# Strassen's seven products for half of the product with w_out in a hybrid decoder layer

## The chip, the cores and the metric

The kernel runs on one core of one Trainium2 chip. The metric is the device time of one execution in microseconds (us); the time of a kernel is the median of its runs. Engines are named as the profile names them: PE is TensorE (matrix products; PEld its weight loads), DVE is VectorE, ACT is ScalarE, POOL is GpSimd, SP issues the loads.

## The reference

One decoder layer over 256 tokens of 1024 channels, in float32: a SwiGLU block, then an SSD branch and a differential attention branch side by side, merged by gates, then a second SwiGLU block. The change is in the line that multiplies the merged branches by `w_out`, and its neighbours:

```python
def rmsnorm(x, g):
    xf = x.astype(jnp.float32)
    y = xf * lax.rsqrt(jnp.mean(xf * xf, axis=-1, keepdims=True) + EPS)
    return y.astype(x.dtype) * g

    ...
        merged = gates[:, :, 0] * y_ssd + gates[:, :, 1] * y_att
        h = h + rmsnorm(merged @ w_out[l], mix_post_g[l])
        h = h + 0.5 * rmsnorm(swiglu(rmsnorm(h, ffn2_pre_g[l]), ffn2_w_gate[l], ffn2_w_up[l], ffn2_w_down[l]),
                              ffn2_post_g[l])
```

`merged` is 256 x 1024 and `w_out` 1024 x 1024.

## The kernel before

**Number format.** Products run in TensorE's rounded float32. To keep float32's precision every operand is split into a high part (rounded) and a low part (the rest), and a product is the sum of three: high x high, low x high, high x low. For weights ScalarE makes the high part (`whi`, L259) and VectorE the low part (`wlo`, L260), each in two operations of 128x1024 for a chunk of 1 MB. For activations ScalarE casts and VectorE subtracts in `split` (L320, L321).

**Weights.** All chunks stand in one list in the order of their use. `load_to` (L241) issues a chunk's load on SP's queue when one of three raw buffers comes free, which is when the low part of the chunk three places earlier has been made. `take` hands the next unit's split weights to the products and splits those up to `AHEAD` = 3 units ahead. The split weights and most activations lie in a pool of 29 tiles (`k4`); small ones in pools of 4 and 7 (`k3`, `k2`). PSUM's eight banks are a pool of three (`pj`) and one of five (`bg`).

**Order.** From the gates on, TensorE's queue is in the order in which the program states it (`own_order(PE)`); the other engines' orders are made by a scheduler when the program is built. An engine works off its own order, and where its next instruction waits, all behind it wait.

**The stage.** The two branches' products (`pws`, `pwd`) leave TensorE in halves of 512 channels and blocks of 128 tokens. VectorE multiplies such a tile by its gate (L1612) and adds the other branch's (L1613), in place in `gt`. `turn_merged` has TensorE transpose a merged tile (`pmg`, L1596) and splits the result into `mh` and `ml`, the activations of the product with w_out. The first half's two tiles are turned after the first weights of the second half's `pwd`, the second half's two within the product with w_out.

`mm_n` computes that product: `acc[b][q]` is the 128-token block b and the 512-column half q, four banks of `bg`. The chunk of the first 256 channels is multiplied for both blocks at once, with the two later transposes between its steps; the other three chunks (`TAIL` = 3) are held, first for block 0, then for block 1:

```python
        for q in range(2):
            for i, w in held:
                one(i, w, ((0, (q,)),), late=not norms or q == 1 or i < n - 1)
```

`ready(0)` then computes block 0's norm while TensorE does block 1: the squares on ScalarE (L506), the gain product on VectorE (`og`, L605), the root on GpSimd (L511, L512), h on VectorE (L645). `turned` has TensorE transpose block 0's h (`pu_f`, L520) ahead of the last third of the stage, for FFN2's first products (`pn_f`); block 1's h is normalized (`un_f`, L565) and transposed within them.

**Strassen elsewhere.** Both SwiGLU blocks' down products already use seven products for eight on three groups of 512 channels each. `Quad` makes the sums of weight quarters on VectorE (`wt`, L122), their high part on ScalarE (`wqh`, L130) and low part on VectorE (`wql`, L136); `sums_of` makes the sums of activation quarters (`sv`, L737 to L740) and splits them (`sh`, `sl`, `s`).

Of the kernel before, what the change touches and what calls it, by code (L numbers as in the profile page):

```python
# [47 lines left out]
SSD_US = 1.55  # L48
DOWN = {"f1": "q1 p q2 p q3 ppp", "f2": "q1 p q2 p q3 ppp"}
FIRST, LAST = (1, 2, 3, 5, 7, 6, 4), (1, 6, 7, 2, 3, 5, 4)  # L50
BREAK, STOP = object(), object()


@with_exitstack
def tile_hybrid_layer(ctx: ExitStack, tc: tile.TileContext, x, ffn1_pre_g, ffn1_w_gate, ffn1_w_up,
# [33 lines left out]
    def bg(shape, name):  # L89
        return ps.tile(shape, F32, tag="bg", name=name, bufs=5)  # L90


    class Quad:
# [32 lines left out]
        def split(self, p):  # L126
            load_to(self.i + 2)
            hi = k4([P, 2, 512], f"wqh{self.i}{p}", F32R)
            src = self.quarter(self.PLAIN[p], p) if p in self.PLAIN else self.sum_of(p)
            nc.scalar.copy(hi, src)  # L130
            rest = self.products[self.products.index(p) + 1:]
            for later in rest[:1] + tuple(q for q in rest[1:2] if p == 3 and q == 4):
                if later in self.SUMS:
                    self.sum_of(later)
            lo = k4([P, 2, 512], f"wql{self.i}{p}", F32R)
            nc.vector.tensor_sub(lo, src, hi.bitcast(F32))  # L136
            self.give_back()
            return lambda kt: hi[:, kt, :], lambda kt: lo[:, kt, :]
# [74 lines left out]
    for c in range(2):  # L213
        for k0 in (0, 512):
            s_chunk(da_w_branch[0], k0, c * 512)
    for c in range(4):
        n_chunk(w_out[0], c * 2 * P)
    ffn_chunks("f2", ffn2_w_gate, ffn2_w_up, ffn2_w_down)

# [187 lines left out]
    def act_table(name):  # L407
        f = nc.scalar.preload_act_table_set(name)
        for prev in act_since:
            tc.add_manual_dep(f.ins, prev, order, reason="activation table")  # L410
        act_since.clear()
        act_fence[0] = f.ins.name
# [317 lines left out]
    def sums_of(g, even, odd):  # L730
# [11 lines left out]
        split(more[:, 0], more[:, 1], v[:, 3])  # L742
        return ([hi[:, i] for i in range(3)] + [more[:, 0]], [lo[:, i] for i in range(3)] + [more[:, 1]])

    def mm_quads(acts, sums, tag):


        bank = {p: bg([P, 512], f"acc_{tag}p{p}") for p in (2, 3, 5, 4, 8)}
        bank.update({p: pj(f"acc_{tag}p{p}") for p in (1, 6, 7)})
        acc = [[bank[2], bank[3]], [bank[4], bank[8]]]  # L750
        begun, n_quads = set(), max(n for n, (kind, j) in enumerate(down[tag]) if kind == "q") + 1
        of_quads = down[tag][:n_quads]

        def mm(p, x_, w_, last):
            nc.tensor.matmul(bank[p], x_, w_, start=p not in begun, stop=last and p in (1, 5, 6, 7))  # L755
            begun.add(p)

        for n, (kind, j) in enumerate(of_quads):
            last = n == n_quads - 1
            if kind == "p":  # L760
                wh, wl = take()
                for kt in range(2):
                    ah, al = acts[2 * j + kt]
                    for b in range(2):
                        ts = slice(b * P, (b + 1) * P)
                        for x_, w_ in ((ah, wh), (al, wh), (ah, wl)):
                            for q in range(2):
                                p = ((2, 3), (4, 8))[b][q]
                                mm(p, x_[:, ts], w_(kt)[:, halves[q]], False)
                continue  # L770
            sh, sl = sums[j]
            for p in LAST if last else FIRST:
                wh, wl = take()
                for kt in range(2):
                    if p in (1, 2, 4):
                        k, b = {1: (0, 0), 2: (2, 0), 4: (2, 1)}[p]
                        ah, al = (x_[:, b * P:(b + 1) * P] for x_ in acts[4 * j + k + kt])
                    else:
                        ah, al = (x_[{5: 0, 6: 1, 7: 2, 3: 3}[p]][:, kt, :] for x_ in (sh, sl))
                    for x_, w_ in ((ah, wh), (al, wh), (ah, wl)):  # L780
                        mm(p, x_, w_(kt), last and kt == 1 and w_ is wl)
            sums[j] = None
        p1, u2, u3, u4, c4 = (k2([P, 512], f"{n}_{tag}") for n in ("p1", "u2", "u3", "u4", "c4"))
        add = lambda o, a, b: nc.vector.tensor_tensor(o, a, b, ALU.add)

        def combine():
            nc.scalar.copy(p1, bank[1])
            m = add(u2, bank[6], p1)
            tc.add_manual_dep(m.ins, last_wlo[0].name, order, reason="behind the last chunk's weights")
            add(u3, bank[7], u2)  # L790
            add(u4, bank[5], u2)
# [794 lines left out]
    yh = yl = None  # L1586
    while turned_pairs[0] < 2:
        back.run(0.1)
    mg, merges = [], []

    def turn_merged(n):

        for q, b, t, mh, ml in merges[:n]:
            pt = bg([P, 4, P], f"pmg{q}{b}")
            for m in range(4):
                nc.tensor.transpose(pt[:, m, :], t[:, m * P:(m + 1) * P], ident)  # L1596
            bs = slice(b * P, (b + 1) * P)
            split(mh[:, :, bs], ml[:, :, bs], pt)
        del merges[:n]

    def attended():
        back.drain()
        act_table(SILU)

    for q in range(2):
        mh = k4([P, 4, T], f"mh{q}", F32R)
        ml = k4([P, 4, T], f"ml{q}", F32R)
        mg += [(mh[:, m, :], ml[:, m, :]) for m in range(4)]

        def merge(b, acc):  # L1610
            t0, t1 = gt[0][b][:, halves[q]], gt[1][b][:, halves[q]]
            nc.vector.tensor_tensor(t1, acc, t1, ALU.mult)  # L1612
            nc.vector.tensor_tensor(t1, t1, t0, ALU.add)  # L1613
            merges.append((q, b, t1, mh, ml))

        natural(f"pwd{q}", 2, lambda j: oh[j // 4][:, j % 4, :], lambda j: ol[j // 4][:, j % 4, :], merge,
                SSD_US if q == 0 else 0.0, (attended, lambda: turn_merged(2))[q])

    pg = load_gain(mix_post_g, "pg_mx")
    acc = [[bg([P, 512], f"acc_mx{b}{q}") for q in range(2)] for b in range(2)]  # L1620

    made, ready, turned = next_norm("f2", "f2")

    def mixed(b):
        n = {}
        for q in range(2):
            norm_half(n, b, q, acc[b][q], pg, 1.0, "mxp")
        norm_end(n, b, 1.0, "mxp")
        ready(b)

    mm_n(acc, mg, mixed, turned, lambda: turn_merged(1))


    norm = made[0]
# [36 lines left out]
```

## Time and profile before

| | |
|---|---|
| Time, median of 3 runs | 730.15 us (730.0 to 730.5) |
| The profiled execution | 731.22 us, span 729.3 us |
| TensorE busy | 721.3 us (99%), 4025 products |
| VectorE busy | 608.5 us (83%) |
| ScalarE busy | 472.8 us (65%) |
| GpSimd busy | 31.5 us (4%) |
| Granted TensorE clock, mean | 0.997 |
| Loaded from memory | 136.17 MB, 188 GB/s over the span |

The span runs from the first to the last instruction of the profiled execution, and times in the views count from its start. A line of a group or of a timeline names the source line (L260 is line 260 of the kernel before), the engine, the operation, the tiles written and read, and their shape; "x3" is three operations in a row, whose length then is that from the first's start to the last's end. A bracket gives the engine's idle time just before and what ended it. A matmul's length in the timeline (0.39 us) is longer than the distance to the next, as they are pipelined.

### The profile page before, as it was taken

The page shows a single profiled execution, that of the slowest core. Times are in us where ns is not written, and L with a number is a line of the kernel's source. Part 1 is how long each engine was busy: PE and PEld are TensorE (multiplying, and loading weights), DVE is VectorE, ACT ScalarE, POOL GpSimd, SP SyncE. Part 2 cuts the span into 40 slices and gives each one's busy share as a digit, 9 for nine tenths or more (in the row PEclk, how much of TensorE's full clock was granted, in tenths as well). Part 3 has the DMA queues.
Part 4 walks back from the last instruction along what each step waited for, and adds up shares of the span by engine and source line. Part 5 has one row for each costly group of instructions (what it writes and reads, how often), then busy time and mean ns, then how long its engine had stood idle before and what let it go on. Part 6 is the DMA issues. An engine that isn't in the chain of part 4 may idle for free.

```text
span 729.3 us, 10568 instructions
## 1 busy us (share of the span) xinstructions
PE 721.3 (99%) x4025; PEld 620.5 (85%) x4025; DVE 608.5 (83%) x933; ACT 472.8 (65%) x804; POOL 31.5 (4%) x63
## 2 busy tenths in 40 slices
PE   9999999999999999999999999999999999999996
PEld 8888888888778889999888788888888888888885
DVE  6978788999979989777996998785784878789996
ACT  6657666666867676869965577782563756566562
POOL 4300000000200000000000000000010000000000
PEclk9999999999999999999999999999999999999998
DMA  8884654467674557665564664465461655654551
GB/s 303 229 275 153 208 173 176 170 231 260 185 227 119 172 173 238 208 213 180 155 224 147 205 224 137 152 235 199 120 234 51 230 182 166 231 194 156 174 197 58
DMA packets 94450, 137.92 MB, mean 189 GB/s; under 512 B 2668, under 2 KB 68800, under 8 KB 94400
## 3 DMA queue, kind: packets, MB, share of 16 engines
q1 hardware_dynamic: 91728, 129.51, 53.7%
q0 software_dynamic: 2368, 7.22, 3.3%
q8 instruction: 31, 0.51, 0.3%
q10 hardware_dynamic: 304, 0.53, 0.2%
q14 instruction: 19, 0.16, 0.1%
HBM read 136.17 MB, written 1.08 MB: 188 GB/s over the span
## 4 chain that ended last, share of the span: by engine, by line
PE 95%; DVE 2%; DMA 1%; issue 1%; ACT 0%; DVEq 0%; ACTq 0%
PE pup_f L341 14%; PE pg_f L341 14%; PE pxs L341 6%; PE pws L382 6%; PE pgt L382 6%; PE acc_f2p L755 5%; PE acc_f1p L755 3%; PE pbc L341 3%; PE pk L341 3%; PE pq L341 3%; PE pn_f L398 3%; PE acc_mx L676 3%; PE pn_mx L382 3%; PE pn_f L382 3%; PE pwd L382 3%; PE pz L333 2%
## 5 line engine op out<-in xcount | busy, mean ns | idle before, releaser
L260 DVE TENSOR_TENSOR wlo<-raw,whi 128x1024 fp32r<-128x1024 f32 x216 | 257.0, 1219 | 20.2 <-ACT whi L259 19.0
L259 ACT CAST whi<-raw 128x1024 fp32r<-128x1024 f32 x216 | 218.4, 1049 | 16.1 <-DMA raw<-in_w_in_dram 5.7
L341 PE MATMUL pg_f<-u_f,whi 128*128 128x512 f32 x288 | 69.0, 390 | 0.0
L341 PE MATMUL pup_f<-u_f,whi 128*128 128x512 f32 x288 | 68.7, 391 | 0.0
L341 PEld LDWEIGHTS pg_f<-u_f,whi 128*128 128x128 f32 x288 | 53.9, 188 | 11.1
L341 PEld LDWEIGHTS pup_f<-u_f,whi 128*128 128x128 f32 x288 | 52.9, 188 | 10.2
L130 ACT CAST wqh<-wt 128x1024 fp32r<-128x1024 f32 x24 | 25.2, 1055 | 23.5 <-DVE wt L122 23.4
L341 PEld LDWEIGHTS pg_f<-u_f,wlo 128*128 128x128 f32 x288 | 36.9, 191 | 1.4
L341 PE MATMUL pup_f<-u_f,wlo 128*128 128x256 f32 x288 | 37.5, 283 | 0.0
L341 PE MATMUL pg_f<-u_f,wlo 128*128 128x256 f32 x288 | 37.4, 283 | 0.0
L347 ACT COPY su_f<-pup_f 128x256 f32<-128x256 f32 x36 | 13.2, 372 | 36.1 <-PE pup_f L341 36.1
L341 PEld LDWEIGHTS pup_f<-u_f,wlo 128*128 128x128 f32 x288 | 35.9, 192 | 0.0
L348 DVE TENSOR_TENSOR su_f<-pup_f,su_f 128x256 f32<-128x256 f32 x36 | 15.2, 421 | 24.2 <-ACT su_f L347 24.1
L382 PE MATMUL pgt<-whi,u_mx 128*128 128x512 f32 x128 | 33.1, 393 | 0.0
L341 PE MATMUL pxs<-u_mx,whi 128*128 128x512 f32 x128 | 31.8, 394 | 0.0
L330 PE MATMUL pz<-u_mx,whi 128*128 128x256 f32 x128 | 31.6, 284 | 0.0
L331 PE MATMUL pz<-u_mx,whi 128*128 128x256 f32 x128 | 31.5, 283 | 0.0
L136 DVE TENSOR_TENSOR wql<-wt,wqh 128x1024 fp32r<-128x1024 f32 x24 | 29.1, 1217 | 0.2
L382 PEld LDWEIGHTS pgt<-whi,u_mx 128*128 128x128 f32 x128 | 23.6, 188 | 5.3 <-issue 0.7
L341 PEld LDWEIGHTS pxs<-u_mx,whi 128*128 128x128 f32 x128 | 23.2, 189 | 4.3
L320 ACT CAST gh_f<-sg_f 128x512 fp32r<-128x512 f32 x18 | 11.2, 620 | 23.2 <-DVE sg_f L911 23.2
L136 DVE TENSOR_TENSOR wql<-raw,wqh 128x1024 fp32r<-128x1024 f32 x18 | 21.8, 1219 | 3.5 <-ACT wqh L130 3.5
(415 smaller groups left out, 1585.1 us busy)
## 6 DMA issues: line engine op xcount, KB each, us to landing
raw<-in_w_in_dram SPq DMA_DIRECT2D x40, 1024.0 KB, 5.1
raw<-in_ffn_w_down_dram SPq DMA_DIRECT2D x22, 1024.0 KB, 4.9
raw<-in_ffn_w_gate_dram SPq DMA_DIRECT2D x20, 1024.0 KB, 5.4
raw<-in_ffn_w_up_dram SPq DMA_DIRECT2D x20, 1024.0 KB, 5.2
raw<-in_ssd_w_branch_dram SPq DMA_DIRECT2D x8, 1024.0 KB, 5.0
acb<-acd POOLq DMA_DIRECT2D x8, 512.0 KB, 4.1
raw<-in_da_w_branch_dram SPq DMA_DIRECT2D x4, 1024.0 KB, 5.1
raw<-in_w_out_dram SPq DMA_DIRECT2D x4, 1024.0 KB, 5.1
```

The source lines that it names most:

```text
L130: nc.scalar.copy(hi, src)
L136: nc.vector.tensor_sub(lo, src, hi.bitcast(F32))
L259: last_cast[0] = behind(nc.scalar.copy(hi, r[:, js, :]), "cast").ins
L260: m = nc.vector.tensor_sub(lo, r[:, js, :], hi.bitcast(F32))
L330: nc.tensor.matmul(acc[m], wh(j)[:, cs], ah(k0 + j), start=first and j == ks[0], stop=False)
L331: nc.tensor.matmul(acc[m], wh(j)[:, cs], al(k0 + j), start=False, stop=False)
L341: nc.tensor.matmul(to, w_(j)[:, m * P:(m + 1) * P], x_(j), start=first and j == 0, stop=not first and j == KD - 1, skip_group_check=True)
L348: nc.vector.tensor_tensor(dst, acc[:, :T], dst, ALU.add)
L382: nc.tensor.matmul(acc, a(k0 + j), b(j), start=first and i == 0, stop=last and i == 11)
L398: nc.tensor.matmul(accs[b], x_(k0 + j), w_(j), start=first and j == 0 and w_ is wh and x_ is acts[b][0], stop=last and j == 3 and w_ is wl)
L676: nc.tensor.matmul(acc[b][q][:, cs] if to is None else to, x_[:, ts], w_(kt)[:, halves[q]][:, cs], start=to is not None and kt == 0 and x_ ...
L755: nc.tensor.matmul(bank[p], x_, w_, start=p not in begun, stop=last and p in (1, 5, 6, 7))
```

## The change

The first 512 of the product's 1024 channels (two of the four chunks of w_out) become one `Quad`, with its own order of the seven products (`MIXED`); `mm_mixed` takes the place of `mm_n`. The five products of 1, 6, 2, 5 and 3 come first, with the two later transposes of merged tiles behind products 6 and 2. Then block 0's plain products of the other 512 channels are accumulated on the banks of products 2 and 3, and block 0's norm begins; products 7 and 4 come behind them, and then block 1's plain products on bank 4 and a new bank 8. The partial products are combined on VectorE (`add`) and in `half_mixed`, which adds the rest to a bank's contents before the norm reads it. `turn_first` turns the first half's two merged tiles and also copies them unsplit (`mt`), from which `sums_of` makes the activations' sums. `of_piece` is the choice of operands that `mm_quads` had inline.

```diff
+MIXED = (1, 6, 2, 5, 3, 7, 4)
...
-    for c in range(4):
+    quad(w_out[0], 0, MIXED)
+    for c in range(2, 4):
         n_chunk(w_out[0], c * 2 * P)
...
+    def of_piece(p, kt, acts, sh, sl):
+
+        if p in (1, 2, 4):
+            k, b = {1: (0, 0), 2: (2, 0), 4: (2, 1)}[p]
+            return [x_[:, b * P:(b + 1) * P] for x_ in acts[k + kt]]
+        return [x_[{5: 0, 6: 1, 7: 2, 3: 3}[p]][:, kt, :] for x_ in (sh, sl)]
+
+    def mm_mixed(acts, sums, turn_next, half, done, turned):
+
+
+        bank, begun = {}, set()
+        sh, sl = sums
+        rest = {n: k2([P, 512], f"{n}_mx") for n in ("p1", "u2", "u4", "u3", "c4")}
+        add = lambda o, p, u: nc.vector.tensor_tensor(rest[o], bank[p], rest[u], ALU.add)
+
+        def mm(p, x_, w_, stop):
+            nc.tensor.matmul(bank[p], x_, w_, start=p not in begun, stop=stop)
+            begun.add(p)
+
+        def piece(p, w):
+            if p not in bank:
+                bank[p] = pj(f"acc_mxp{p}") if p in (1, 6, 7, 4) else bg([P, 512], f"acc_mxp{p}")
+            wh, wl = w
+            for kt in range(2):
+                ah, al = of_piece(p, kt, acts[:4], sh, sl)
+                for x_, w_ in ((ah, wh), (al, wh), (ah, wl)):
+                    mm(p, x_, w_(kt), kt == 1 and w_ is wl and p in (1, 5, 6, 7))
+
+        def plain(b, q, p, i, w):
+            wh, wl = w
+            for kt in range(2):
+                ah, al = (x_[:, b * P:(b + 1) * P] for x_ in acts[4 + 2 * i + kt])
+                for x_, w_ in ((ah, wh), (al, wh), (ah, wl)):
+                    mm(p, x_, w_(kt)[:, halves[q]], i == 1 and kt == 1 and w_ is wl)
+
+        piece(1, take())
+        nc.scalar.copy(rest["p1"], bank[1])
+        piece(6, take())
+        turn_next()
+        add("u2", 6, "p1")
+        piece(2, take())
+        turn_next()
+        piece(5, take())
+        add("u4", 5, "u2")
+        piece(3, take())
+        late = [(p, take()) for p in (7, 4)]
+        ws = [take() for _ in range(2)]
+        for q, (p, o) in enumerate(((2, "p1"), (3, "u4"))):
+            for i, w in enumerate(ws):
+                plain(0, q, p, i, w)
+            half(0, q, bank[p], rest[o])
+        done(0)
+        split_to(ahead_of(taken[0], AHEAD - 2))
+        split_to(ahead_of(taken[0], AHEAD - 1))
+        for p, w in late:
+            piece(p, w)
+            if p == 7:
+                add("u3", 7, "u2")
+                add("c4", 5, "u3")
+        bank[8] = pj("acc_mxp8")
+        for q, (p, o) in enumerate(((4, "u3"), (8, "c4"))):
+            for i, w in enumerate(ws):
+                if q == 1 and i == 0:
+                    turned()
+                plain(1, q, p, i, w)
+            half(1, q, bank[p], rest[o])
+        split_to(ahead_of(taken[0], AHEAD))
+        done(1)
...
     def turn_merged(n):
...
             split(mh[:, :, bs], ml[:, :, bs], pt)
+            if q == 0:
+                nc.scalar.copy(plain_mg[0][:, :, bs], pt)
         del merges[:n]
...
+    def turn_first():
+        plain_mg.append(k4([P, 4, T], "mt"))
+        turn_merged(2)
+        sums_mg.append(sums_of(0, plain_mg[0][:, 0:2, :], plain_mg[0][:, 2:4, :]))
...
-                SSD_US if q == 0 else 0.0, (attended, lambda: turn_merged(2))[q])
+                SSD_US if q == 0 else 0.0, (attended, turn_first)[q])
...
-    acc = [[bg([P, 512], f"acc_mx{b}{q}") for q in range(2)] for b in range(2)]
...
+    norms_mx = [{}, {}]
+
+    def half_mixed(b, q, acc, rest):
+        nc.vector.tensor_tensor(rest, acc, rest, ALU.add)
+        norm_half(norms_mx[b], b, q, rest, pg, 1.0, "mxp")
 
     def mixed(b):
-        n = {}
-        for q in range(2):
-            norm_half(n, b, q, acc[b][q], pg, 1.0, "mxp")
-        norm_end(n, b, 1.0, "mxp")
+        norm_end(norms_mx[b], b, 1.0, "mxp")
         ready(b)
 
-    mm_n(acc, mg, mixed, turned, lambda: turn_merged(1))
+    mm_mixed(mg, sums_mg[0], lambda: turn_merged(1), half_mixed, mixed, turned)
```

More of the change, by code (lines that the diff above doesn't have):

```diff
@@ L774, in mm_quads @@
                 for kt in range(2):
[L775 to L779, printed above, removed]
+                    ah, al = of_piece(p, kt, acts[4 * j:4 * j + 4], sh, sl)
                     for x_, w_ in ((ah, wh), (al, wh), (ah, wl)):
@@ L1588, in tile_hybrid_layer @@
         back.run(0.1)
-    mg, merges = [], []
+    mg, merges, plain_mg, sums_mg = [], [], [], []
     def turn_merged(n):
```

## The prediction

> **What bounds the kernel now.** I read the page first (busy time, then the chain of work that ended last), then the chain in order of time around the product with w_out, then a table of stretches, then VectorE's and ScalarE's timelines there.
>
> ```profile
> PE 721.3 (99%) x4025; PEld 620.5 (85%) x4025; DVE 608.5 (83%) x933; ACT 472.8 (65%) x804; POOL 31.5 (4%) x63
> ...
> PE 95%; DVE 2%; DMA 1%; issue 1%; ACT 0%; DVEq 0%; ACTq 0%
> ```
>
> ```profile
> 493.00:519.70 26.70, 26.70 (x127) 22.18 (x126) 13.81 (x19) 8.88 (x12) 0.53 (x1) 1.00 0.34 127
> 519.70:543.40 23.70, 23.70 (x114) 19.67 (x113) 20.28 (x29) 16.13 (x30) 1.91 (x4) 1.00 0.79 265
> ...
> 567.00:722.00 155.00, 155.00 (x823) 134.18 (x822) 132.44 (x168) 93.94 (x136) 0.63 (x1) 1.00 0.54 184
> ```
>
> The first fence is the page, the second a table of stretches (busy time of TensorE, its weight loads, VectorE, ScalarE and GpSimd, then the granted clock). TensorE is busy in the whole of every stretch and carries 95% of the chain: whatever leaves its queue saves its own time, and whatever makes it wait is added in full. The pair to watch is the third after the stretch's length, VectorE (DVE): in 519.7 to 543.4, the stage of this change, it is busy 20.28 of 23.70 us and has 3.4 us left; in the stretch before it has 12.9 us left. The last stretch, FFN2, has TensorE busy 155.00 of 155.00 us, so a delay cannot be given back there.
>
> The chain in order of time gives TensorE's prices (start, length, work):
>
> ```profile
> 519.87 2.73 PE acc_mx L676 x12
> 522.60 0.44 PE pmg L1596 x4
> ...
> 526.23 12.29 PE acc_mx L676 x54
> ...
> 543.53 8.16 PE pn_f L382 x36
> 551.69 0.87 PE pu_f L520 x8
> ```
>
> One 128x512 product costs 12.29/54 = 0.228 us, four transposes 0.44. The stage starts at 519.87 and FFN2's first products (pn_f) at 543.53; block 1's transposes follow at 551.69, all without a wait.
>
> VectorE's and then ScalarE's timeline (start, length, engine, line, operation, tiles; in brackets the idle time before):
>
> ```profile
> 505.42 0.69 DVE L1612 TENSOR_TENSOR gt<-pwd,gt 128x512 f32<-128x512 f32 x1 [5.59 <-PE pwd L382]
> ...
> 514.63 1.29 DVE L321 TENSOR_TENSOR ml<-pmg,mh 128x512 fp32r<-128x512 f32 x2 [5.08 <-ACT mh L320]
> 516.07 2.36 DVE L260 TENSOR_TENSOR wlo<-raw,whi 128x1024 fp32r<-128x1024 f32 x2
> 518.35 0.68 DVE L1612 TENSOR_TENSOR gt<-pwd,gt 128x512 f32<-128x512 f32 x1
> ...
> 520.08 0.68 DVE L1613 TENSOR_TENSOR gt<-gt,gt 128x512 f32<-128x512 f32 x1
> ...
> 528.66 3.49 DVE L260 TENSOR_TENSOR wlo<-raw,whi 128x1024 fp32r<-128x1024 f32 x3
> ```
>
> ```profile
> 514.02 1.07 ACT L320 CAST mh<-pmg 128x512 fp32r<-128x512 f32 x2 [16.11 <-PE pmg L1596]
> ...
> 523.07 0.59 ACT L320 CAST mh<-pmg 128x512 fp32r<-128x512 f32 x1 [4.19 <-PE pmg L1596]
> ```
>
> Here is the slack that matters. The second channel half's first transposes (pmg at 522.60) need the merged gt, whose last operation (L1613) runs at 520.08 to 520.76: 1.8 us to spare. Between the two ml and that operation stand two wlo, the multiply of L1612 and one more wlo. Back to back, a 128x1024 VectorE operation costs (3.49-1.22)/2 = 1.135 us, and two 128x512 ones 1.29 us, so 0.60 for the first.
>
> **The change part by part.**
>
> *TensorE's work.* The plain form has, for 512 channels, 4 (128-channel steps) x 2 (token blocks) x 2 (halves) x 3 (split terms) = 48 products; seven products of quarters over two steps and three terms are 42. The other 512 channels keep 48. So 96 become 90: 6 x 0.228 = 1.37 us saved. Nothing else leaves the queue.
>
> *VectorE's work.* In place of eight wlo there are four sums of raw quarters (wt), seven wql and four wlo, that is seven more 128x1024 operations; also four sums of the activations (sv), their two low parts (sl, s), and eight additions of partial products. FFN1 and FFN2 have the same forms:
>
> ```profile
> L122 DVE TENSOR_TENSOR wt<-raw 128x1024 f32<-128x1024 f32 x6 | 7.3, 1217 | 0.0
> L136 DVE TENSOR_TENSOR wql<-wt,wqh 128x1024 fp32r<-128x1024 f32 x24 | 29.1, 1217 | 0.2
> L738 DVE TENSOR_TENSOR sv<-sg_f x6: 414/416/417, 50.7 to 631.4; 128x256 f32<-128x256 f32 x6
> L321 DVE TENSOR_TENSOR sl<-sv,sh x6: 949/951/957, 57.8 to 637.5; 128x768 fp32r<-128x768 f32 x6
> ```
>
> wt and wql cost what wlo does (1.217), sv 0.42 and s, of the same size, the same, sl 0.95; back to back, less the 0.085 by which 1.22 exceeds 1.135. Added: 7 x 1.135 + 5 x 0.34 + 0.87 + 8 x 0.60 = 15.3 us. Two wt and four wql stand ahead of the first merge in the built program's order: four operations more than before, 4.5 us into the 5.59 us idle time before 505.42. These are hidden. The other 10.8 us come after 514, where before had about 3.4 us.
>
> *The stall that decides.* The scheduler fixes VectorE's order when the program is built; in it, after the two ml, come three sv, wt, sv, sl, s, wt, wql, the L1612 multiply, two wql, two wlo, and only then the L1613 addition of block 0. The second pair of ml ends at 514.63+1.29 = 515.92. The copy of the merged block to mt is queued on ScalarE behind that ml (0.59, the length of an mh cast), so sv starts at 516.57. Then 4 x 0.34 + 0.87 + 0.34 + 7 x 1.135 + 0.60 + 0.69 = 11.8: the addition ends at **528.4**, not 520.8.
>
> ```profile
> 519.71 0.62 PE L676 MATMUL acc_mx<-whi,mh 128*128 128x512 f32 x2
> ```
>
> TensorE begins piece 1 at 519.87 and ends it at 521.24. Piece 6 is given the bank of piece 1 (both come from the pool of three), so it waits for ScalarE's copy of that bank: 0.59 and the refill of the array, 0.16 (the chain counts the first product from 519.87, the timeline issues it at 519.71): **0.8 us**. Piece 6 ends at 523.4. The next in TensorE's queue are the transposes of the merged gt, so all products behind them wait to 528.4: **5.0 us**, although pieces 2, 5 and 3 need nothing of it. Then 0.44 and piece 2, to 530.2; block 1's merged gt is three operations further (0.60+1.135+0.69): 530.7, **0.5 us**.
>
> *The norm of block 0.* From 531.2 TensorE does pieces 5 and 3 and 24 plain products (36 x 0.228), to 539.4, then pieces 7 and 4 and 12 plain ones, to 544.85, where it transposes h. Behind 530.64 VectorE is never idle: wlo, ml, u2, wlo, ml, u4, and the wlo that ends at 536.5. That frees the buffer for FFN2's fourth load:
>
> ```profile
> L259 ACT CAST whi<-raw 128x1024 fp32r<-128x1024 f32 x216 | 218.4, 1049 | 16.1 <-DMA raw<-in_w_in_dram 5.7
> ...
> raw<-in_ffn_w_up_dram SPq DMA_DIRECT2D x20, 1024.0 KB, 5.2
> ```
>
> ```profile
> DMA to landing us min/median/max: 4.8/5.1/6.2
> ```
>
> The load takes 5.2 to land, so 541.7; its cast (1.05) stands on ScalarE ahead of the square of block 0's second half, L506. The norms' steps, as block 0 (L645, L528) and block 1 (the rest) have them now:
>
> ```profile
> 536.43 1.41 DVE L645 SCALAR_TENSOR_TENSOR h<-og_mxp,rp_mxp,h 128x512 f32<-128x512 f32 x2 [0.27 <-POOL rp_mxp L512]
> ...
> 540.38 2.16 DVE L528 SCALAR_TENSOR_TENSOR u_f<-pu_f,cols_a,u_f 128x128 fp32r<-128x128 f32 x8 [0.34 <-ACT u_f L526]
> ...
> 548.97 1.03 DVE L565 TENSOR_SCALAR un_f<-h,r_f 128x512 f32<-128x512 f32 x2 [1.89 <-POOL r_f L512]
> ```
>
> ```profile
> 543.62 0.60 ACT L506 ACTIVATE jp_mxp<-acc_mx 128x512 f32<-128x512 f32 x1 [0.36 <-PE acc_mx L676]
> 544.12 0.19 ACT L506 ACTIVATION_READ_ACCUMULATOR jp_mxp<-acc_mx 128x1 f32 x1
> ```
>
> ```profile
> 544.41 0.57 POOL L511 TENSOR_SCALAR rp_mxp<-sp_mxp 128x1 f32<-128x1 f32 x1 [4.69 <-ACT jp_mxp L506]
> 545.06 0.56 POOL L512 TENSOR_TENSOR rp_mxp<-rp_mxp,small 128x1 f32<-128x1 f32 x1
> ```
>
> The square takes 0.60+0.19 = 0.79, the root on GpSimd 1.21 (544.41 to 545.62), and h its 1.41, from 544.7 to 546.1 instead of 537.84. TensorE transposes its second half from there and so waits **0.6 us** in all. VectorE has ended its other work by then (13.3 us from 530.64, to 544.0).
>
> *The norm of block 1.* After h VectorE has two additions, two wlo, one addition, one gain product, and the eight u_f of 2.16: 546.0 + 0.60 + 1.135 + 0.60 + 1.135 + 0.60 + 2.1 = 552.2. Only then the last addition c4 (0.69, to 552.9), then square, root, h, square, root and un as now: from the square at 543.62 to the start of un at 548.97 were 5.35 us, and half of un's 1.03 goes by until its first half is there: 558.8. TensorE has transposed h (0.44 behind 546.1), done the last 12 plain products (2.73) and 36 of pn_f (8.16) by 557.5: **1.3 us**. From here every step stands as before, FFN2's weights included, which are split as far ahead of their products as now.
>
> *The sum.* 0.8 + 5.0 + 0.5 + 0.6 + 1.3 = 8.2, less 1.37: +6.8. Counted directly, the transposes of un come at 558.8 in place of 551.69, +7.1. I take **+6.9**. The profiled execution took 731.22 us (span 729.3, and 1.9 around it), 1.07 above the median of 730.15; the sum is made against 731.22 (738.1) and moved to the median: **737.0 us**. 0.2% is 1.46 us, about what a measurement of this kernel can tell from no change.
>
> Bounds of the unknown: bank 1's copy is not in the trace; if it cost nothing the sum is 0.8 lower, if it stood behind one more cast (1.05) that much higher, of which block 0's and 1's waits would hide half. VectorE runs from 516.6 to 558 with hardly a gap, so 2% in its lengths is 0.8 us either way. The weights' waits for TensorE to release buffers name products that are long over, and cost nothing; landings that take 6.2 instead of 5.2 add up to 1.0 at h.
>
> **TensorE's clock** may not stay full over a 5 us gap. The stretches after the last product (it ends at 723.2), and the first products of the kernel, show it:
>
> ```profile
> 723.30:725.50 2.20, 0.00 (x0) 0.00 (x0) 1.85 (x6) 1.04 (x5) 0.00 (x0) 1.00 0.00 0
> 725.60:729.30 3.70, 0.00 (x0) 0.00 (x0) 0.74 (x2) 0.00 (x0) 0.00 (x0) 0.50 0.37 142
> ```
>
> ```profile
> 1.11 2.93 PE L475 MATMUL warm<-zeros 128*128 128x128 f32 x12 [1.11 <-DVE zeros L455]
> ...
> 4.17 1.11 PE L957 MATMUL pu_f<-ident,h 128*128 128x128 f32 x4
> ...
> 6.89 0.60 PE L957 MATMUL pu_f<-ident,h 128*128 128x128 f32 x4
> ```
>
> The granted clock is 1.00 for 2.2 us after the last product and 0.50 behind it. At the start four transposes took 1.11 us at 4.17 and 0.60 at 6.89: nearly half speed for some 4 us after the first product. So half speed may set in some 2 us before TensorE resumes at 528.4, and 4 us of it lose 2. But TensorE has waits of 0.5, 0.6 and 1.3 us ahead of it, 2.4 in all, set by VectorE and what hangs on it, and a later TensorE waits that much less there: nothing is added to the end.
> [...]
>
> **The rivals.**
>
> *A: the sums fit (faster).* If VectorE reached the L1613 addition before TensorE ended piece 6 (523.4), the stalls would go, and 1.37 us less the 0.8 of bank 1 be left: 729.6, or 728.8 if that copy were hidden too. For it: VectorE's 12.9 idle us before 519.7. Against: the operations between ml and addition are 11.8 us, and the point from which it decides is 6.8 us. The order is fixed and the lengths have rows.
>
> *B: half speed outlasts the cover.* If it lasts 7 to 10 us instead of 4 it loses 3.5 to 5, less the cover of 2.4: 738.1 to 739.6. For it: the gap is longer than the 2.2 us of full clock at the end. Against: 4 us at the start, and the cover. [...]
>
> *C: only the 5 us wait comes.* If the norms' steps find more room than I count (h's wait on the load, un's on c4), 0.8 + 5.0 + 0.5 less 1.37 remain, +4.9, or less if VectorE's hand-overs are quicker: 733 to 735. Against: VectorE has 10.8 us more to do in a stretch in which it had 3.4 left.
>
> **How the numbers follow.** Forecast 0.78, for 735.4 to 738.8: -1.6 (bank 1's copy free, VectorE 2% faster) and +1.8 (VectorE 2% slower, a landing of 6.2). A 0.05, B 0.10, C 0.07. With half of B and a little of C the range is **735.0 to 739.2**, which leaves out less than 2 in 10. A lies at -0.6 to -1.4 and beyond if VectorE frees more, so its 0.05 goes in 0.02 faster and 0.03 the same; slower 0.95.
>
> **What would show it.** Right: in the changed profile TensorE has 6 fewer products of w_out, an idle time of about 5 us ahead of the second pair of pmg, released by VectorE's gt addition, 0.8 us ahead of piece 6 released by the copy p1, and shorter waits ahead of pu_f twice; VectorE over 20 us busy without a gap from 516.6; FFN2's stretch as long as now. Wrong: if pmg's wait is under 3 us, if the gt addition ends before 526, if TensorE's products after the gap show 0.45 us each beyond 535, or if FFN2 gives time back.

## The result, and the profile after

The changed kernel takes **738.36 us** (median of 4 runs, 737.93 to 738.99), the kernel before, run beside it, 730.33 us: +8.0 us, a ratio of 1.0109 with a 95% interval of 1.0094 to 1.0124. The prediction was 737.0 us in a range of 735.0 to 739.2, and slower.

The first line of the page of the changed kernel (busy time and instructions of each engine), and the table of stretches of its trace, with the columns as in the prediction:

```profile
PE 722.6 (98%) x4019; PEld 621.2 (84%) x4019; DVE 623.6 (85%) x954; ACT 479.2 (65%) x812; POOL 30.7 (4%) x63
```

```profile
513.00:519.70 6.70, 6.70 (x34) 5.60 (x32) 5.39 (x10) 4.45 (x7) 0.51 (x1) 1.00 0.09 17
519.70:534.00 14.30, 8.69 (x33) 6.62 (x32) 14.30 (x17) 9.82 (x12) 0.02 (x1) 0.76 0.87 288
534.00:550.00 16.00, 16.00 (x76) 13.35 (x75) 14.97 (x20) 9.96 (x21) 0.88 (x2) 1.00 0.67 228
574.00:729.00 155.00, 155.00 (x824) 134.22 (x823) 132.52 (x168) 93.75 (x136) 0.63 (x1) 1.00 0.53 184
```

TensorE has six matmuls fewer (4019 after 4025) and VectorE is busy 15.1 us longer (623.6 after 608.5). FFN2's stretch is as it was, 155.00 of 155.00 us. Most of the loss arises in the second line: there VectorE has no idle time left in 14.30 us, TensorE works 8.69 of them, at a mean granted clock of 0.76.

TensorE's timeline in the stage, the rows in which it waited or ran slowly (start, length, line, tiles; in brackets the idle time before and who ended it), then VectorE's up to the addition for which TensorE waits:

```profile
520.93 0.50 PE L763 MATMUL acc_mxp<-wqh,sh 128*128 128x512 f32 x1 [0.68 <-ACT p_mx L783]
527.53 1.09 PE L1663 MATMUL pmg<-ident,gt 128*128 128x128 f32 x4 [4.94 <-DVE gt L1687]
528.84 0.63 PE L763 MATMUL acc_mxp<-wqh,ml 128*128 128x512 f32 x1
529.27 0.63 PE L763 MATMUL acc_mxp<-wql,mh 128*128 128x512 f32 x1
...
530.98 1.05 PE L1663 MATMUL pmg<-ident,gt 128*128 128x128 f32 x4
...
545.52 1.03 PE L522 MATMUL pu_f<-ident,h 128*128 128x128 f32 x8
...
558.21 1.09 PE L522 MATMUL pu_f<-ident,un_f 128*128 128x128 f32 x8 [0.74 <-DVE un_f L567]
```

```profile
515.60 0.43 DVE L739 TENSOR_TENSOR sv<-mt 128x256 f32<-128x256 f32 x1 [0.65 <-ACT mt L1667]
...
519.29 1.22 DVE L123 TENSOR_TENSOR wt<-raw,wt 128x1024 f32<-128x1024 f32 x1
520.42 1.22 DVE L137 TENSOR_TENSOR wql<-raw,wqh 128x1024 fp32r<-128x1024 f32 x1
521.56 0.69 DVE L1686 TENSOR_TENSOR gt<-pwd,gt 128x512 f32<-128x512 f32 x1
522.16 2.35 DVE L137 TENSOR_TENSOR wql<-wt,wqh 128x1024 fp32r<-128x1024 f32 x2
524.43 2.35 DVE L262 TENSOR_TENSOR wlo<-raw,whi 128x1024 fp32r<-128x1024 f32 x2
526.70 0.69 DVE L1687 TENSOR_TENSOR gt<-gt,gt 128x512 f32<-128x512 f32 x1
```

This is the stall of the prediction row by row: VectorE does not pause from 515.60 to 540.13, the merge addition ends at 527.39, and TensorE stands until 527.53. Behind the stall the products come 0.43 us apart instead of 0.228.

The first product of the stage starts at 518.73 here and at 519.71 in the profile before. In all traces of this case TensorE has the same products ahead of the stage, and it starts between 518.73 and 520.59 without following the changes, so that much of a run's time is scatter. A sharper measure is the **stage's length**, from its first product to the transposes of block 1 (pu_f from un_f): 31.82 us before (519.71 to 551.53), **39.48** now (518.73 to 558.21), +7.66. From there to the end of TensorE's last product it is 171.7 to 171.9 us in all traces but two (e3 and e5, explained below). Its ends, in the profile before and in the changed kernel's (the other two rows are shown in the prediction and above):

```profile
551.53 1.03 PE L520 MATMUL pu_f<-ident,un_f 128*128 128x128 f32 x8
```

```profile
518.73 0.39 PE L763 MATMUL acc_mxp<-wqh,mh 128*128 128x512 f32 x1
```

### The profile page after: what moved, and what is told of

Same layout as the page of the kernel before. It is cut to its first block, busy times and chain, and to the rows that moved or that the text cites. A ratio compares the mean times of both kernels' runs of the same rounds, so it can differ in the third digit from the quotient of the medians.

```text
span 736.2 us, 10589 instructions
## 1 busy us (share of the span) xinstructions
PE 722.6 (98%) x4019; PEld 621.2 (84%) x4019; DVE 623.6 (85%) x954; ACT 479.2 (65%) x812; POOL 30.7 (4%) x63
## 5 line engine op out<-in xcount | busy, mean ns | idle before, releaser
L262 DVE TENSOR_TENSOR wlo<-raw,whi 128x1024 fp32r<-128x1024 f32 x212 | 252.5, 1220 | 17.1 <-ACT whi L261 16.7
L261 ACT CAST whi<-raw 128x1024 fp32r<-128x1024 f32 x212 | 214.4, 1048 | 15.1 <-DMA raw<-in_w_in_dram 3.3
L131 ACT CAST wqh<-wt 128x1024 fp32r<-128x1024 f32 x28 | 29.3, 1054 | 25.1 <-DVE wt L123 20.9
L137 DVE TENSOR_TENSOR wql<-wt,wqh 128x1024 fp32r<-128x1024 f32 x28 | 33.9, 1220 | 0.2
L137 DVE TENSOR_TENSOR wql<-raw,wqh 128x1024 fp32r<-128x1024 f32 x21 | 25.5, 1220 | 3.3 <-ACT wqh L131 3.3
```

The source lines that it names most:

```text
L261: last_cast[0] = behind(nc.scalar.copy(hi, r[:, js, :]), "cast").ins
L262: m = nc.vector.tensor_sub(lo, r[:, js, :], hi.bitcast(F32))
```

## The experiments

Theory V: VectorE's work in the 20 us behind the first transposes sets the pace: it has more to do there than there is time for, and TensorE waits wherever it first needs something of VectorE's queue. Rivals: that products stand in TensorE's queue behind a transpose they don't need (O); the half clock (H); the banks, or the pieces themselves. All were timed against the kernel before on the same chip:

| kernel | us | before | ratio and 95% interval | stage's length |
|---|---|---|---|---|
| changed kernel | 738.36 | 730.33 | 1.0109 (1.0094 to 1.0124) | 39.48 |
| e1, transposes later | 739.97 | 731.21 | 1.0125 (1.0112 to 1.0138) | 41.15 |
| e2, merge first | 739.06 | 731.21 | 1.0114 (1.0101 to 1.0127) | 40.31 |
| e3, no low parts | 735.94 | 731.21 | 1.0069 (1.0056 to 1.0082) | 35.55 |
| e4, split early | 732.52 | 731.21 | 1.0029 (1.0017 to 1.0041) | 33.13 |
| e5, spare products | 738.61 | 731.31 | 1.0101 (1.0085 to 1.0116) | 39.16 |
| e6, early and thinned | 729.75 | 731.31 | **0.9982** (0.9974 to 0.9991) | 30.40 |
| e7, before with more VectorE | 735.46 | 731.31 | 1.0057 (1.0045 to 1.0070) | 36.40 |
| e8, other bank | 738.58 | 731.31 | 1.0103 (1.0089 to 1.0117) | 39.15 |
| e9, e6 and six products | 731.23 | 731.15 | 1.0004 (0.9995 to 1.0013) | 31.76 |
| e10, thinned only | 737.28 | 731.15 | 1.0082 (1.0068 to 1.0096) | 38.13 |

The intervals are about 1 us wide on each side; what lies closer together than that is told apart by the stage's length, from one trace each. That trace is of the slowest execution for e3 and e5, and of the fastest for the changed kernel and e8.

### e1: the transposes later in TensorE's queue

```diff
         piece(6, take())
-        turn_next()
         add("u2", 6, "p1")
         piece(2, take())
-        turn_next()
         piece(5, take())
         add("u4", 5, "u2")
         piece(3, take())
+        turn_next()
+        turn_next()
```

> Only TensorE's order changes: the two groups of transposes of the second merged half stand behind pieces 2, 5 and 3 instead of ahead of 2 and 5. Theory V (VectorE's amount of work between 514 and 534 sets the pace, in whatever order TensorE asks): pieces 1, 6, 2, 5 and 3 then end at about 526.5, the transposes still wait for the merge addition at 527.4, and the low part of the first transposed block stands behind two more weight splits on VectorE, so the plain products of block 0 begin at 534.9 as in the changed kernel (534.64): 738 to 740 us. Rival O (what costs is that products which need nothing stand behind a waiting transpose): the 5 us wait shrinks to about 1, and 733.5 to 735 us. Rival H (half clock after the gap costs 2 us of its own): 736 if the gaps stay under 2.3 us each.

739.97 us: no gain. TensorE's timeline:

```profile
528.26 0.63 PE L1663 MATMUL pmg<-ident,gt 128*128 128x128 f32 x4 [0.86 <-DVE gt L1687]
530.60 1.08 PE L1663 MATMUL pmg<-ident,gt 128*128 128x128 f32 x4 [1.71 <-DVE gt L1687]
532.74 0.80 PE L763 MATMUL acc_mxp<-whi,mh 128*128 128x512 f32 x1 [1.06 <-ACT mh L322]
535.71 0.79 PE L763 MATMUL acc_mxp<-whi,ml 128*128 128x512 f32 x1 [2.17 <-DVE ml L323]
```

The single wait of 4.94 us became four, of 5.8 us together, and the last one is again for VectorE (ml). VectorE's queue, made anew from the changed program, has the low part of the transposed block behind still more splits, and block 0's first product with it comes no sooner (16.24 us behind the stage's first product, 16.14 in the changed kernel). Work put ahead of a wait only helps if the next thing waited for comes no later. O falls.

The half clock has a part in this time: the granted clock was 0.50 for 10.24 us, from 530.5, although no wait was longer than 2.17 us, so rival H's condition (full clock if the gaps stay under 2.3) did not hold. Twelve products behind the last wait took 5.16 us instead of 2.74. At full clock the stage would have been 38.8 us by this (an estimate: 16.24, and the 22.6 that TensorE works from there on in the changed kernel), still not O's gain of 3 us and more.

### e2: the merge first in VectorE's queue

```diff
-            w = take()
+            w = take(2 if i and name == "pwd1" else AHEAD)
```

This is in the loop of `natural`; the splits of pieces 3, 7 and 4 and of a plain chunk are then issued behind the merge.

> The same work on VectorE in another order: the sums and splits of the pieces 3, 7 and 4 and of the first plain chunk are issued behind the two merge additions. Theory V: the addition of block 0 ends at about 520, so the transposes wait for nothing and pieces 2, 5 and 3 follow at once, but the low part of the transposed block ends only at about 531.4, as now, and TensorE waits there instead, some 4 us in two parts ahead of block 0's plain products: about 736.2 us (735 to 737.5). Rival O (the place of the addition in VectorE's order is the whole cost): the 5 us go and nothing takes their place, 731.5 to 733 us.

739.06 us: 2.9 us above theory V's number (0.9 of it the chip's, where before took 731.21), and 6 and more above O's. VectorE's and TensorE's rows:

```profile
518.98 0.69 DVE L1687 TENSOR_TENSOR gt<-gt,gt 128x512 f32<-128x512 f32 x1
...
526.45 4.63 DVE L262 TENSOR_TENSOR wlo<-raw,whi 128x1024 fp32r<-128x1024 f32 x4
530.99 0.69 DVE L323 TENSOR_TENSOR ml<-pmg,mh 128x512 fp32r<-128x512 f32 x1
```

```profile
528.82 0.50 PE L763 MATMUL acc_mxp<-whi,mh 128*128 128x512 f32 x1 [2.02 <-ACT mh L322]
531.74 0.80 PE L763 MATMUL acc_mxp<-whi,ml 128*128 128x512 f32 x1 [2.41 <-DVE ml L323]
...
559.20 1.09 PE L522 MATMUL pu_f<-ident,un_f 128*128 128x128 f32 x8 [2.00 <-DVE un_f L567]
```

The addition now starts at 518.98 instead of 526.70, and no transpose waits. The 4.4 us stand ahead of block 0's plain products instead, where the low part of the transposed block comes behind the operations that were moved, at 530.99 (530.77 in the changed kernel). What V's number missed lies further on: two of FFN2's low parts slipped between c4 and h in VectorE's order, and beside them GpSimd's first step of block 1's root takes 2.05 us instead of 0.30 (e4 has the rows), so that block 1's wait is 2.00 us instead of 0.74. So putting the merge first did not save its wait: the same work stands ahead of the next thing that TensorE needs.

### e3: seven operations fewer on VectorE

```diff
-            lo = k4([P, 2, 512], f"wql{self.i}{p}", F32R)
-            nc.vector.tensor_sub(lo, src, hi.bitcast(F32))
+            if self.products is MIXED and p in NO_LOW:
+                lo = hi
+            else:
...
```

`NO_LOW` names all seven pieces. The kernel leaves out these low parts, so its result is not the layer's; only its time is of use.

> Left out: the low parts of the seven pieces' weights; the products that used them run with the high part in their place, so that TensorE has as many products and VectorE seven 128x1024 operations (7.9 us) fewer, in the same order. Theory V: the addition comes five operations sooner (about 522), no wait of TensorE at the transposes is left, and the time is about 732.8 us (732 to 734), with 0.8 us ahead of piece 6 and some 1 to 2 us ahead of block 1's transposes still there. Rival B (bank, weights' loads or the half clock make the time): over 735 us.

735.94 us, 3.1 us above V's number (0.9 of it the chip's), with a stage 3.9 us shorter than in the changed kernel. TensorE's waits that are left:

```profile
529.96 0.50 PE L767 MATMUL acc_mxp<-whi,ml 128*128 128x512 f32 x1 [0.23 <-DVE ml L327]
...
556.14 1.61 PE L526 MATMUL pu_f<-ident,un_f 128*128 128x128 f32 x8 [3.27 <-DVE un_f L571]
```

The wait at the transposes is gone, as V has it (0.68 us ahead of piece 6 stays), but 3.27 us of it return ahead of block 1's transposes: with TensorE on time, block 1's norm on VectorE, ScalarE and GpSimd is next. The half clock that follows this wait costs another 1.6 us: from here to the last product are 173.4 us, not 171.8. By the time alone rival B (over 735 us) would hold. The trace tells them apart: the waits that V takes away are gone, and the half clock, one of B's causes, has a share of 1.6 us in the traced execution.

### e4: the pieces split early

```diff
-            w = take()
+            w = take((3.75, 2.75)[i] if name == "pwd1" else AHEAD)
```

The number counts chunks of four quarters; 3.75 reaches all seven pieces.

> The same work, issued sooner: at the first chunk of the last product before the stage all seven pieces are split ahead (15 quarters ahead instead of 12), so that two sums and three low parts can run in VectorE's 5.1 us of idle time before 513.7 instead of behind it. Theory V: the work behind 514 falls by 5.7 us, the transposes and the plain products wait for nothing, and about 1 us is left ahead of block 1's transposes: about 731.8 us (730.8 to 733.5). Rival S (the buffers for the early pieces aren't free before the products of the stage ahead are done, so nothing moves): 737 to 739 us.

732.52 us, 0.7 above V's number and inside its range. The first line is from the table of stretches, the others are TensorE's:

```profile
493.00:513.00 20.00, 20.00 (x94) 16.54 (x93) 18.95 (x22) 9.02 (x11) 0.00 (x0) 1.00 0.49 177
```

```profile
522.38 0.60 PE L1663 MATMUL pmg<-ident,gt 128*128 128x128 f32 x4
...
552.78 1.09 PE L522 MATMUL pu_f<-ident,un_f 128*128 128x128 f32 x8 [2.57 <-DVE un_f L567]
```

In the changed kernel the same stretch reads:

```profile
493.00:513.00 20.00, 20.00 (x94) 16.54 (x94) 12.64 (x15) 5.66 (x7) 0.00 (x0) 1.00 0.17 69
```

VectorE is now busy 18.95 of the 20 us ahead of the stage instead of 12.64, and all waits up to block 1's transposes are gone, that ahead of piece 6 too. The likely reason for the last is that with the multiply (L1686) sooner in VectorE's order, piece 6 is given the bank that it frees, not that of piece 1 (e2 has it sooner as well, and no such wait); the views don't name the bank. What is left is 2.57 us, more than the 1.37 that the six products save. Most of it is GpSimd's first step of block 1's root, beside two low parts on VectorE:

```profile
546.03 2.12 POOL L513 TENSOR_SCALAR rp_mxp<-sp_mxp 128x1 f32<-128x1 f32 x1 [1.09 <-ACT jp_mxp L508]
```

```profile
545.03 1.22 DVE L262 TENSOR_TENSOR wlo<-raw,whi 128x1024 fp32r<-128x1024 f32 x1
546.16 0.69 DVE L607 TENSOR_TENSOR og_mxp<-c_mx,pg_mx 128x512 f32<-128x512 f32 x1
546.76 1.22 DVE L262 TENSOR_TENSOR wlo<-raw,whi 128x1024 fp32r<-128x1024 f32 x1
```

The step takes 0.30 us in the changed kernel, which has no low part there, and ends here 0.17 us behind the second low part.

### e5: TensorE kept busy in its wait

```diff
...
         piece(6, take())
+        spare = bg([P, 512], "spare_mx")
+        for _ in range(18):
+            nc.tensor.matmul(spare, acts[0][0][:, 0:P], w1[0](0), start=True, stop=True)
         turn_next()
```

(`w1` is the weights of piece 1.)

> The changed kernel with 18 spare 128x512 products (4.1 us) into a bank of their own behind piece 6, so that TensorE is busy for most of its 5 us wait and its clock stays full; nothing else differs. Step of the prediction under test (half speed loses some 2 us, but waits further on take it up): the products behind the transposes go back from 0.43 to 0.228 us apart, the waits at the second transposes and ahead of block 1's transposes grow by as much, and the time is within 0.7 us of the changed kernel's 738.4. Rival H (half speed is paid at the end): 736 to 736.5 us.

738.61 us, as expected; the stage is 39.16 us long, 0.3 shorter.

```profile
523.31 4.26 PE L788 MATMUL spare_mx<-wqh,mh 128*128 128x512 f32 x18
528.42 0.63 PE L1667 MATMUL pmg<-ident,gt 128*128 128x128 f32 x4 [0.85 <-DVE gt L1691]
...
530.76 0.63 PE L1667 MATMUL pmg<-ident,gt 128*128 128x128 f32 x4 [0.32 <-DVE gt L1691]
...
558.78 1.09 PE L522 MATMUL pu_f<-ident,un_f 128*128 128x128 f32 x8 [1.98 <-DVE un_f L567]
```

With the clock full (1.00 from 522.60 to 545.00), TensorE's products go at 0.228 us again, a wait of 0.32 us appears at the second transposes, and block 1's wait grows from 0.74 to 1.98 us. The waits take up what the clock gave, and H falls in this place. It is not the clean test that was meant, though: the scheduler made other orders too. Block 0's h starts 22.74 us behind the first product instead of 25.46, and a low part that stood ahead of c4 stands behind it, where GpSimd's step takes 0.99 us instead of 0.30. So the 0.3 us is the net of these.

### e6 and e10: early, and the rest of the queues thinned

To e4's edit, e6 adds in `mm_mixed`:

```diff
-        piece(1, take())
+        piece(1, take(2.5))
...
-        late = [(p, take()) for p in (7, 4)]
-        ws = [take() for _ in range(2)]
+        late = [(p, take(2)) for p in (7, 4)]
+        ws = [take(2) for _ in range(2)]
...
-        split_to(ahead_of(taken[0], AHEAD))
+        steps = split_steps()
+        next(steps)
         done(1)
+        normed["lo"] = norms_of[1]["h"]
+        for _ in steps:
+            pass
+        normed["cast"] = last_sq[0]
```

(Pieces 6, 2, 5 and 3 have the 2.5 too; `last_sq` is the latest square on ScalarE; `normed` makes later low parts and casts follow the named instruction.) e10 has these lines without e4's edit.

> The pieces split early as in the run before that did so, and also VectorE's and ScalarE's queues thinned in the two places that were left: the plain chunks and FFN2's first chunks are split later (two chunks ahead instead of three), one half of FFN2's third chunk and all of its fourth come behind block 1's norm on VectorE, and the fourth's casts behind block 1's squares on ScalarE. Theory V (with VectorE out of the way the change is worth its 1.37 us): the 2.57 us wait of the split-early run ahead of block 1's transposes goes, and the time is 1 to 1.4 us below the kernel before on the same chip. Rival (the longer chain of block 1's norm, with its extra addition and the eight gain products ahead of it, can't be hidden behind 36 products): 1 us or more of that wait stays and the time is at best that of before.

> The thinned queues without the early split of the pieces: the merge addition then stands behind the same late operations as in the changed kernel. Theory V: the 5 us wait at the transposes and the half clock behind it stay, only block 1's wait goes: 737 to 738 us, 0.5 to 1.5 us below the changed kernel. Rival (the thinned queues are what brought the gain): 733 us or less.

e6 takes **729.75 us**, 0.18% (0.09 to 0.26) below the kernel before: faster than both kernels. Its stretches, and TensorE at block 1's transposes:

```profile
519.70:534.00 14.30, 14.30 (x69) 11.84 (x68) 14.30 (x20) 9.42 (x13) 0.00 (x0) 1.00 0.56 178
534.00:550.00 16.00, 16.00 (x76) 13.36 (x75) 13.54 (x24) 10.12 (x27) 4.80 (x9) 1.00 0.33 108
```

```profile
550.30 1.04 PE L522 MATMUL pu_f<-ident,un_f 128*128 128x128 f32 x8
```

TensorE has no idle time, and the stage is 30.40 us long, 1.42 less than before; six products are 1.37. The low parts are now behind block 1's h, and GpSimd's first step takes 0.30 us again. e10 takes 737.28 us and still has the big wait:

```profile
528.49 0.82 PE L1668 MATMUL pmg<-ident,gt 128*128 128x128 f32 x4 [4.93 <-DVE gt L1692]
```

So the thinned queues alone bring some 1.4 us of stage, the early split 6.3 (39.48 to 33.13), and both are needed to get below the kernel before.

### e9: the six products back

```diff
+        spare = bg([P, 512], "spare_mx")
+        for _ in range(6):
+            nc.tensor.matmul(spare, acts[0][0][:, 0:P], w1[0](0), start=True, stop=True)
         piece(6, take(2.5))
```

> The faster kernel of the run with the thinned queues, with six spare 128x512 products between pieces 1 and 6, as many as the seven products of quarters leave out: TensorE has the work of the plain form again, everything else stays. Theory V (TensorE is the bound again in that kernel, and the saving is those six products): 6 x 0.228 = 1.4 us slower than it, that is within 0.4 us of the kernel before. Rival (the gain came from the thinned queues and not from the products): as fast as it, 1.4 us or more below before.

731.23 us against 731.15: no difference from the kernel before, and a stage of 31.76 us (31.82 before). What e6 gains is the six products and nothing else.

### e7: the kernel before with more work on VectorE

```diff
-            m = nc.vector.tensor_sub(lo, r[:, js, :], hi.bitcast(F32))
+            for _ in range(2 if i in DOUBLED else 1):
+                m = nc.vector.tensor_sub(lo, r[:, js, :], hi.bitcast(F32))
```

> The kernel before, with the low parts of four chunks (the last three of w_out and the first of FFN2) made twice over: eight 128x1024 operations, 9.1 us, more on VectorE in about the stage of the change, and none elsewhere. Theory V (the stage has room for some 3.4 us of VectorE, what goes beyond it turns into waits of TensorE): 3 to 6 us slower than before, with waits at the second transposes and ahead of the products with the late low parts. Rival (the loss comes from the pieces themselves: their bank, their order, their longer chain of additions): at most 1 us slower.

735.46 us, 4.2 more than before, without any piece, sum or extra bank:

```profile
527.68 0.66 PE L1598 MATMUL pmg<-ident,gt 128*128 128x128 f32 x4 [2.28 <-DVE ml L323]
```

So VectorE's load alone, 9.1 us of it, costs half of what the changed kernel loses with 15.3 us, of which 10.8 fall into this stretch. The 2.28 us are the only wait of TensorE in this trace's stage, and most of the rest of the 4.6 us by which it is longer is the half clock behind the wait (3.41 us, which cost some 1.7).

### e8: another bank for piece 6

```diff
-                bank[p] = pj(f"acc_mxp{p}") if p in (1, 6, 7, 4) else bg([P, 512], f"acc_mxp{p}")
+                bank[p] = pj(f"acc_mxp{p}") if p in (1, 7, 4) else bg([P, 512], f"acc_mxp{p}")
```

> The changed kernel with piece 6 in the pool of five banks, so that it doesn't wait for the copy of piece 1. The 0.8 us idle time ahead of piece 6 goes, and by theory V the wait at the transposes that follow becomes as much longer (5.7 us), since the merge addition is what ends it: within 0.4 us of the changed kernel. If the bank's wait counts by itself: 0.8 us faster.

738.58 us, a stage of 39.15.

```profile
527.84 1.08 PE L1663 MATMUL pmg<-ident,gt 128*128 128x128 f32 x4 [5.92 <-DVE gt L1687]
```

The wait ahead of piece 6 is gone, and the one behind it has grown by 0.98: a wait that ends at a time set elsewhere swallows what is saved ahead of it.

## Why the prediction was right, and where it was off

- **TensorE's six products, 1.37 us.** Right; in the changed kernel they are hidden behind waits, in e6 and e9 they are worth 1.4 us.
- **VectorE's load and the merge addition, 5.0 us.** Right: the addition ends 8.66 us behind the stage's first product (527.39 - 518.73), predicted 8.69 (528.4 - 519.71), the wait is 4.94, and e4 and e7 show that the load makes it, from both sides. The order of VectorE's queue, on which the working rests, tells where TensorE waits; e2 shows that another order, with the merge first, cost as much, which the prediction did not say.
- **Bank of piece 6, 0.8 us.** The bubble is there: 520.93 is 0.83 behind the end of piece 1 (518.73 + 6 x 0.228 = 520.10): the row of its last product ends at 520.26, 0.16 later, and the copy takes 0.59 from 520.29. No row shows what the 0.16 is, which the prediction calls the refill of the array. As the sum had it, the 5.0 us begin only behind it, and e8 shows that it is no price of its own.
- **The second transposes (0.5) and block 0's norm (0.6).** Neither wait shows: half speed made TensorE late enough. For the second the wrong cause was named, too (below).
- **Half clock.** It set in 2.5 us behind the last product and lasted 6.8 us (the granted clock is 1.00 to 525.10 and 0.50 from 525.20 to 531.90). The four transposes and six products behind the wait, the second transposes and one product took 4.61 us (527.53 to 532.14) where the same in e4 takes about 2.5: 2.1 us, as estimated. That the waits further on take it up fits e5, whose stage is 0.3 us shorter at full clock (with the other orders named there). The clock was halved in all three traces in which TensorE had this gap (4.94 us in the changed kernel, 5.92 in e8, 4.93 in e10): the products behind it come 0.43 us apart in each. The price at the end was that of the waits.
- **Block 1's norm, 1.3 us.** 0.74 with TensorE 2 us late; 1.98 in e5 with TensorE on time, 0.7 of it GpSimd's longer step. The working names one addition behind h more than it sums; the changed profile has what it sums.
- **The step that was mis-sized** is block 0's h. The working let the cast ahead of the second square start when FFN2's load lands, 22.0 us behind the first product (541.7 - 519.71), and said that the weights' waits for TensorE's buffers cost nothing. ScalarE's timeline of the changed kernel:

```profile
541.41 1.06 ACT L261 CAST whi<-raw 128x1024 fp32r<-128x1024 f32 x1 [2.26 <-PE acc_mxp L763]
542.37 0.62 ACT L508 ACTIVATE jp_mxp<-u_mx 128x512 f32<-128x512 f32 x1
```

The load was issued at 535.54 and had landed 5.0 us later, at 540.5, 21.8 us behind the first product as predicted. The cast, idle for 2.26 us ahead, is released by piece 7's products, which TensorE's half speed had made late, and starts 22.7 us behind the first product: it writes into a buffer that they still read. So h starts 25.46 us behind it (544.19) instead of 24.99, c4 32.93 (551.66) instead of 32.49, and the transposes 39.48 instead of 39.09.

```profile
544.19 1.42 DVE L647 SCALAR_TENSOR_TENSOR h<-og_mxp,rp_mxp,h 128x512 f32<-128x512 f32 x2 [0.88 <-POOL rp_mxp L514]
...
551.66 0.69 DVE L1699 TENSOR_TENSOR c_mx<-acc_mxp,c_mx 128x512 f32<-128x512 f32 x1
```

From c4 to the transposes the working holds to 0.1 us (6.55 for 6.6). The sum took 6.9 where its own end of the stage gave 7.3 by this reckoning (39.09 - 31.82); with h's 0.4 that is the stage's 7.66, and the rest to the measured 8.0 is within what the runs scatter. The listed waits don't add up to it one by one: two of the five (0.5 and 0.6) didn't come and the half clock's 2.1 stands in their place. The total held because VectorE's chain to un, which the direct count follows, sets the end of the stage.

- **The rivals.** A (the sums fit) is what e4 and e6 made true by other means: the work had to go into VectorE's idle time ahead of the first transposes. The measured 738.36 us lies in B's span (738.1 to 739.6), but not by B's cause: no row ahead of the result shows B's 7 to 10 us of half speed, and the half clock lasted 6.8 us, only some 4.4 of them with TensorE at work, and the waits further on covered them but for the 0.4 us at h. C did not come: block 1's wait is there.

## What to carry to other kernels

A form that trades matmuls for elementwise work is priced on the engine that does the elementwise work, in the stretch where it falls: count that engine's idle time there, and look for the idle time of the stretch before, into which the work can be issued. Moving the waiting instruction, in the one queue or the other, moved the wait (5.8 us of waits in e1 and 4.4 in e2 for the one of 4.94); taking work out of the stretch removed it (e3, e4), and only then were the saved matmuls worth their time (1.42 us of the stage in e6). When the first wait is gone, expect the next chain (here block 1's norm, with GpSimd's step at 2.12 us in e4 instead of 0.30, beside VectorE's low parts) to hold back part of it, and go on until the bounding engine shows no gap.

## What the runs showed of the hardware

The half clock lasted one, two or three times the same length in these traces. The clock records have it for 3.41 us (e5, e7), 6.83 (the changed kernel, e2) or 10.24 (e1). The wait ahead of it differed: the changed kernel's clock fell 2.5 us into a wait of 4.94; in e5 (the table of stretches, granted clock third from the right) a wait of 1.98 us, with eight transposes behind it, came ahead, and the clock fell 1.1 us after TensorE had gone on:

```profile
555.80:559.90 4.10, 2.12 (x14) 1.62 (x13) 1.46 (x3) 2.25 (x7) 1.63 (x3) 1.00 0.56 198
559.95:563.30 3.35, 3.35 (x9) 2.67 (x8) 2.16 (x8) 1.70 (x7) 0.00 (x0) 0.50 0.02 5
```

In e4, the traced execution has a wait of 2.57 us in the same place, and its granted clock is 1.00 in the 6.8 us from 550.20 to 557.00; in e1 the clock fell near the end of the second of two waits, 0.86 and 1.71 us, with four transposes between them. The mean granted clock differs from one execution to the next: e5's four take 737.9 and 738.0 us with 0.998 and more, and 739.2 and 739.9 with 0.997; e4's take 732.0 to 732.4 us with 0.999 and 732.6 to 735.2 with 0.996 or 0.997. In this place TensorE has no wait further on, and the half clock costs 1.6 us (e3: 173.4 us to the last product instead of 171.8); behind the merge's wait the changed kernel's 6.83 us cost at most some 0.4. So in e5 a wait of 1.98 us, the last one ahead of a full queue, cost nearly twice its length (1.98 + 1.6, an estimate) in the executions with the lower clock.

One step on GpSimd took longer where VectorE worked beside it. The first step of the root, on a tile of 128x1, takes 0.30 to 0.31 us in the changed kernel, and 2.05 (e2), 2.12 (e3, e4) and 0.99 us (e5) beside low parts or the gain product; in all four it ends 0.17 us behind VectorE's operation. Why it does is not shown by these runs.
